# Pooling given out one VectorE instruction at a time, under four merge-gate tiles per layer instead of two

## The chip, the cores and the metric

One Trainium2 chip, one of its cores. The time is that of one execution of the whole program on the device, in microseconds (us); a kernel's time is the median of its runs. Engines: TensorE does matmuls (PE in the rows; PEld is its weight load), VectorE is DVE, ScalarE is ACT, GpSimd is POOL, and SyncE (SP) issues the DMAs.

## The reference

Two layers over 1024 latent tokens and 256 context tokens of width 1024, all in float32. A layer normalises its input, multiplies it by one wide matrix `w_in`, and cuts the product into the inputs of four branches, into gates, and into merge gates:

```
z      = split_cols(h @ w_in)            # pool_in, MLA, diff, windowed q/k/v, gates, merge
y_pool = for each of 4 column groups of 64, window w in (2, 4, 8, 16):
           mean of u over the window, minus u, then @ w_pool[group]; times s_pool
y_mla, y_diff, y_swa = three attentions
m      = sum over branches r of sigmoid(merge[r]) * ((y[r] * silu(gates[r])) @ w_br[r])
x      = x + gate * rms_norm(m @ w_out)
```

Layer 0 does this for all 1280 tokens, layer 1 for the 1024 latents (its keys and values still take all 1280).

## The kernel before, in words

**Precision.** A float32 product is three matmuls: each operand is split into a rounded part (ScalarE) and what is left of it (a subtraction on VectorE, for most weight tiles on GpSimd); `mm3` (line 74) issues high by high, high by low, low by high.

**Dense tiles.** `h @ w_in` is done in tiles of 128 output columns. A tile runs over chunks of tokens (512, 512, 256, or 512, 512), each of 8 steps of three matmuls into one of two PSUM buffers `pd`; then ScalarE copies the chunk out. `Dense` (line 319) holds a queue of such tiles in a fixed order. `fill(us)` (line 359) takes steps from the queue until their estimated cost covers `us`; a step of 512 tokens is put at 0.648, one of 256 at 0.324. So a tile is 12.96 of the planner's units over 1280 tokens and 10.37 over 1024. Where the queue is empty, `fill` does nothing. `until(name)` (line 368) runs the queue without a break up to the end of one tile. As a tile starts, the DMA of the next one's weights (512 KB) is issued; their split (rounding on ScalarE, subtraction `wl` on GpSimd) is issued at the next attention unit (line 1252).

**Later work.** `Later` (line 154) holds generators. Every dense step advances its clock by the step's cost, and a generator whose time has come is resumed; what it yields is the delay to its next part. `drain` runs it to its end.

**Order of the queue.** Values, keys and queries of the differential attention, which are run ahead of all attention by `until(W_DQ + 1)` (line 975); then eight gate tiles, the values (SV), keys (SK) and queries (SQ, two tiles) of the windowed attention, the pooling, and two merge-gate tiles (lines 788 to 800). These are given out between the pieces of attention.

**Attention** (lines 1245 to 1275). Units in the order differential, MLA, windowed. A unit has two or four score pieces (matmuls, a row minimum on VectorE, an exponential on ScalarE) and up to five turns (transposes on TensorE, `th` on ScalarE, `tl` on VectorE, matmuls into `acc`). After each piece `fill(f)` gives dense steps; `f` comes from `FILL` and `TURNS`. Ahead of the first piece stand 15 units of dense work in layer 0 and 13 in layer 1. `prefetch(i + 1)`, after a unit's first score piece, issues the DMAs of the next unit's keys, values and queries. For a windowed unit it first calls `dense.until(W_SQ + 1)` if SQ's second tile is not through yet (lines 1220 to 1223):

```python
if key[0] == 3:
    if any(it[0] == W_SQ + 1 for it in dense.items) or dense.gen and dense.name == W_SQ + 1:
        dense.until(W_SQ + 1)
    vals.drain()
```

**Rope.** SQ's second tile, like DQ's, hands each chunk to a chain: two products on VectorE and two on GpSimd, sums on VectorE, rounding on ScalarE, subtraction on VectorE, and four DMAs to DRAM (`ev2`, line 646), from where `prefetch` loads the queries.

**Pooling** (`pooled`, line 724). Two tiles of `pool_in`, each copied to `up` in SBUF; after each tile an item of the queue without a matmul tile, `rest`: for a chunk, window sums by two or four additions, a 64-partition copy, a product with `rcnt` (1 / count, by DMA), a subtraction, the split, and one `mm3` with `w_pool`. It yields twice per chunk, 0.3 and 0.4 units, so a whole chunk is given out at one or two places.

**Merge stage** (lines 1425 to 1476). For each branch r and output tile d the merge-gate tile is projected and the branch product of the tile before is computed and added. A tile in `early` was projected in the attention stage, kept in DRAM (`zmd`), and here is only loaded and put through a sigmoid (`reload`).

The engines' queues run in the order written into the program; a scheduler arranges that order ahead of time from this code's order and from its own estimate of when each instruction can start.

Of the kernel before, what the change touches and what calls it, by code (L numbers as in the profile page):

```python
# [8 lines left out]
F = mybir.dt.float32  # L9
R = mybir.dt.float32r  # L10
# [9 lines left out]
T = SEQ + CTX  # L20
# [12 lines left out]
def kernel(ctx: ExitStack, tc: tile.TileContext, A: dict, out: bass.AP):  # L33
# [46 lines left out]
    def dense_ps(n, m=128):  # L80
        return ps_d.tile([128, 512], F, name="pd", tag="pd")[0:m, 0:n]
# [28 lines left out]
    zmd = dram.tile([2, 128, T], F, name="zmd")  # L110
# [409 lines left out]
    def layer(l, es_prev):  # L520
# [84 lines left out]
        def f32(tag, n):  # L605
            return p2.tile([128, {"t1": 528, "t2": 528}.get(tag, 512)], F, name=tag, tag=tag, bufs=3 if tag == "tab" else 2)[:, 0:n]
# [6 lines left out]
        def spl(src, dh, dl, scale=None):  # L613
            pp = slice(0, src.shape[0])
            n = src.shape[-1]
            hi = p2.tile([128, 512], R, name="sh", tag="sh")[pp, 0:n]
            lo = p2.tile([128, 512], R, name="sl", tag="sl")[pp, 0:n]
            if scale is None:
                act(hi, src)
                tt(lo, src, hi.bitcast(F), ALU.subtract)  # L620
            else:
                act(hi, src, scale=scale)
                stt(lo, src, scale, hi.bitcast(F), ALU.mult, ALU.subtract)
            dh(hi)
            dl(lo)
# [88 lines left out]
                dma(zgd[j, :, c0:c0 + n], z)  # L714
            dense.tile(st, W_G + j, qch, ev)

        def merge_gate(e, i):
            def ev(ps, c0, n):
                z = f32("zc", n)
                act(z, ps)  # L720
                dma(zmd[e, :, c0:c0 + n], z)
            dense.tile(st, i, qch, ev)

        def pooled():
            LP = 8 + SEQ + 8 + CTX + 8
            H_, L_ = slice(64, 128), slice(0, 64)
            wph = p2.tile([128, 2, 128], R, name="wph", bufs=1)
            wpl = p2.tile([128, 2, 128], R, name="wpl", bufs=1)
            spc = p2.tile([128, 2], F, name="spc", bufs=1)
            keep = {}  # L730

            def pos(c0):
                return c0 + 8 if c0 < SEQ else c0 + 16

            def weights():
                wpr = f32("zc", 256).rearrange("p (a b) -> p a b", a=2)
                nc.gpsimd.memset(wpr, 0.0)
                for g in range(4):
                    o = 64 * (g % 2)
                    dma(wpr[o:o + 64, g // 2, o:o + 64], A["w_pool"][l, g])  # L740
                split(wpr, wph, wpl)
                dma(spc, A["s_pool"][l].rearrange("(j p) -> p j", p=128))

            for j in range(2):
                def ev(ps, c0, n, j=j):
                    if c0 == 0:
                        vals.drain()
                        if j == 0:
                            weights()
                        keep[j] = p2.tile([128, LP], F, name="up", tag="zt1", bufs=1)  # L750
                        nc.gpsimd.memset(keep[j], 0.0)
                    act(keep[j][:, pos(c0):pos(c0) + n], ps)
                dense.tile(st, W_POOL + j, qch, ev)

                def rest(j=j):
                    for c0, n in qch:
                        up = keep[j][:, pos(c0) - 8:pos(c0) + n + 8]
                        w = n + 16
                        a = f32("t1", w)
                        b = f32("t2", w)  # L760
                        tt(a[:, 1:w], up[:, 0:w - 1], up[:, 1:w], ALU.add)
                        if j == 0:
                            tt(b[H_, 8:8 + n], a[H_, 7:7 + n], a[H_, 9:9 + n], ALU.add)
                        else:
                            tt(b[:, 2:w - 1], a[:, 1:w - 2], a[:, 3:w], ALU.add)
                            tt(a[:, 4:w - 3], b[:, 2:w - 5], b[:, 6:w - 1], ALU.add)
                            tt(b[H_, 8:8 + n], a[H_, 4:4 + n], a[H_, 12:12 + n], ALU.add)
                        yield 0.3 * n / 512
                        nc.vector.tensor_copy(out=b[L_, 8:8 + n], in_=a[L_, 8:8 + n])
                        rc = f32("tab", n)  # L770
                        dma(rc, A["rcnt"][j, :, c0:c0 + n])
                        t1 = f32("tab", n)
                        tt(t1, b[:, 8:8 + n], rc, ALU.mult)
                        tt(t1, t1, up[:, 8:8 + n], ALU.subtract)
                        hl_ = {}
                        spl(t1, lambda h: hl_.__setitem__(0, h), lambda h: hl_.__setitem__(1, h))
                        ps = dense_ps(n)
                        mm3(ps, lambda k: wph[:, j], lambda k: wpl[:, j], lambda k: hl_[0], lambda k: hl_[1], [0], 1)
                        yv = f32("zc", n)
                        act(yv, ps, scale=spc[:, j:j + 1])  # L780
                        dma(yd[0][j, :, c0:c0 + n], yv)
                        yield 0.4 * n / 512
                dense.add(f"pool{j}", None, rest)


        vals, ups = Later(), Later()
# [4 lines left out]
        roped(W_DQ, dqd.rearrange("m a d n -> a m d n"), qch, 32 ** -0.5, 8, 16, ("C32", "S32"))  # L791
        for j in range(8):
            gates(j)
        values(W_SV, svd, 0)
        keys_swa()
        roped(W_SQ, sqd, qch, 64 ** -0.5, 4, 32, ("C64", "S64"))
        pooled()
        early = [W_M + 26, W_M + 29]
        for e, i in enumerate(early):
            merge_gate(e, i)  # L800

        p1b = pool(f"mlb{l}", 1, es_m)

# [466 lines left out]
        while pend:  # L1270
            dense.fill(1.0)
            pend.pop(0)()
        dense.until(early[-1])
        es_a.close()
        es_p.close()

# [148 lines left out]
        for q, (r, d) in enumerate(order):  # L1425
            i = W_M + r * 8 + d
            if q + 1 == len(order):
                st.load((l, W_O), use=0)
            elif i not in early:
                st.load((l, i + 2 if i + 1 in early else i + 1))  # L1430
# [14 lines left out]
            def ev(ps, c0, n, sg_tile=sg_tile):  # L1445
                act(sg_tile(c0, n), ps, AF.Sigmoid)
# [13 lines left out]
            body = reload(early.index(i)) if i in early else st.body((l, i), qch, ev)  # L1460
            some(body, KT)
            if prev:
                if prev[1] == 0:
# [251 lines left out]
```

## Time and profile before

| | us |
|---|---|
| median of 3 runs (lowest to highest) | 2755.56 (2752.95 to 2758.76) |
| the profiled execution | 2752.83 |
| its span, first to last instruction | 2749.9 |
| TensorE busy in it | 2616.0 (95%) |
| VectorE, ScalarE, GpSimd busy | 1526.6, 1190.7, 801.2 |
| mean granted TensorE clock | 0.973 of full speed |

Attention runs from about 240 to 840 us in layer 0 and from about 1700 to 2220 us in layer 1; the merge stages follow them. A TensorE that is shown as busy can still be slow: where PEclk is below 1.00 in a stretch, part of it ran at the lower of two clocks, half of full speed.

### The profile page before, as it was taken

The numbers are of one execution on the slowest core, as the hardware profiler recorded it, in microseconds if no ns is written. First come the engines' busy times: TensorE is split into PE (matmuls) and PEld (weight loads), VectorE is DVE, ScalarE is ACT, GpSimd is POOL, SyncE is SP. The second block draws the span as 40 slices with busy tenths as digits, with TensorE's granted clock in tenths as the row PEclk, the third lists the DMA queues.
The fourth block names the chain that finished last, engine by engine and source line by source line (L and its number), as shares of the span: only waits on it lengthen the run. The fifth ranks groups of instructions, "written<-read, shape, count | busy, mean of one in ns | idle before, by whom it ended". The sixth has DMA issues, their size and how long they took to land. (4 is left out here: it accounts for less than half of the span.)

```text
span 2749.9 us, 38514 instructions
## 1 busy us (share of the span) xinstructions
PE 2616.0 (95%) x14194; PEld 2205.1 (80%) x14194; DVE 1526.6 (56%) x2638; ACT 1190.7 (43%) x2188; POOL 801.2 (29%) x492
## 2 busy tenths in 40 slices
PE   7998999999999998999999998999998999999998
PEld 5777878888888887888878776888887878888878
DVE  7544778656665686333147653888666642222333
ACT  4433666655474221222245442776554742222231
POOL 4223433111000223444323322443010013344424
PEclk9998999999999999999999998999999999999999
DMA  6376333433334553222125366433433333322223
GB/s 238 103 198 208 116 96 92 115 118 115 94 109 122 170 182 124 77 77 66 54 92 179 101 205 207 133 94 106 136 100 94 112 118 98 98 79 79 79 73 100
DMA packets 211950, 327.00 MB, mean 119 GB/s; under 512 B 27060, under 2 KB 124466, under 8 KB 211762
## 3 DMA queue, kind: packets, MB, share of 16 engines
q1 hardware_dynamic: 211762, 324.55, 38.0%
q8 instruction: 111, 1.82, 0.3%
q14 instruction: 77, 0.63, 0.1%
HBM read 241.43 MB, written 80.22 MB: 117 GB/s over the span
## 5 line engine op out<-in xcount | busy, mean ns | idle before, releaser
L76 PE MATMUL pd<-h,wh 128*128 128x512 f32 (+2 forms) x2288 | 863.1, 377 | 24.6 <-ACT sg L50 11.9
L78 PE MATMUL pd<-h,wl 128*128 128x512 f32 (+2 forms) x2288 | 847.9, 371 | 0.4 <-POOL wl L53 0.4
L77 PE MATMUL pd<-h,wh 128*128 128x512 f32 (+2 forms) x2288 | 846.1, 370 | 0.0
L53 POOL TENSOR_TENSOR wl<-wraw,wh 128x1024 fp32r<-128x1024 f32 x106 | 260.7, 2459 | 926.3 <-ACT wh L50 886.2
L76 PEld LDWEIGHTS pd<-h,wh 128*128 128x128 f32 (+1 forms) x2288 | 437.0, 191 | 87.4 <-ACT sg L50 12.9
L78 PEld LDWEIGHTS pd<-h,wl 128*128 128x128 f32 (+1 forms) x2288 | 435.4, 190 | 70.2 <-POOL wl L53 1.8
L77 PEld LDWEIGHTS pd<-h,wh 128*128 128x128 f32 (+1 forms) x2288 | 437.3, 191 | 57.8 <-DVE h L56 0.8
L998 DVE CUSTOM_DVE_ANT_0 P<-pss,zero 128x1280 f32<-128x1280 f32 (+1 forms) x216 | 295.8, 1370 | 147.0 <-PE pss L1137 75.7
L53 DVE TENSOR_TENSOR tl<-pt,th 128x512 fp32r<-128x512 f32 (+1 forms) x420 | 277.0, 671 | 149.9 <-ACT th L50 146.4
L50 ACT ACTIVATE th<-pt 128x512 fp32r<-128x512 f32 (+1 forms) x420 | 239.6, 581 | 141.8 <-PE pt L1026 136.4
L1026 PE MATMUL pt<-kc,P 128*128 128x128 f32 x1632 | 256.6, 276 | 6.1 <-POOL P L53 1.6
L53 DVE TENSOR_TENSOR sg<-sg,pt 128x512 f32<-128x512 f32 x96 | 65.7, 687 | 349.9 <-PE pt L78 349.4
L1042 PE MATMUL acc<-th,vt 128*128 128x256 f32 x816 | 240.9, 309 | 7.5 <-ACT ot L50 6.6
L1042 PE MATMUL acc<-tl,vt 128*128 128x256 f32 x816 | 219.5, 290 | 16.6 <-DVE tl L53 16.5
L50 ACT ACTIVATE wh<-wraw 128x1024 fp32r<-128x1024 f32 x124 | 130.7, 1054 | 208.7 <-PE pd L77 139.1
L50 ACT ACTIVATE P<-P,m 128x1280 f32<-128x1280 f32 (+1 forms) x144 | 182.8, 1269 | 62.5 <-DVE m L998 62.0
L1026 PEld LDWEIGHTS pt<-kc,P 128*128 128x128 f32 x1632 | 191.6, 141 | 19.1 <-DVE P L56 5.4
L50 ACT ACTIVATE sg<-pd 128x512 f32<-128x512 f32 x120 | 70.9, 591 | 277.4 <-PE pd L78 269.3
L50 ACT ACTIVATE P<-P,negm 128x1280 f32<-128x1280 f32 (+3 forms) x144 | 146.6, 1018 | 95.0 <-DVE negm L998 94.0
L1042 PEld LDWEIGHTS acc<-th,vt 128*128 128x128 f32 x816 | 156.2, 191 | 39.0 <-ACT th L50 18.2
L53 POOL TENSOR_TENSOR m<-m,sg 128x512 f32<-128x512 f32 x96 | 131.0, 1371 | 190.8 <-DVE sg L53 189.9
L1042 PEld LDWEIGHTS acc<-tl,vt 128*128 128x128 f32 x816 | 156.2, 191 | 34.5 <-DVE tl L53 25.7
(293 smaller groups left out, 3946.5 us busy)
## 6 DMA issues: line engine op xcount, KB each, us to landing
wraw<-in_w_in_dram SPq DMA_DIRECT2D x108, 512.0 KB, 3.6
wmt<-in_w_modt_dram SPq DMA_DIRECT2D x64, 256.0 KB, 3.1
wraw<-in_w_out_dram SPq DMA_DIRECT2D x32, 512.0 KB, 3.3
yd<-ot SPq DMA_DIRECT2D x108, 128.0 KB, 2.0
kt<-dkd SPq DMA_DIRECT2D x64, 160.0 KB, 3.9
qt<-dqd SPq DMA_DIRECT2D x72, 128.0 KB, 2.8
ya<-yd SPq DMA_DIRECT2D x36, 256.0 KB, 3.1
yb<-yd SPq DMA_DIRECT2D x36, 256.0 KB, 3.0
```

The costliest lines, as they stand in the source:

```text
L50: return nc.scalar.activation(out=o, in_=i, func=func, **kw)
L53: return (e or nc.vector).tensor_tensor(out=o, in0=a, in1=b, op=op)
L76: nc.tensor.matmul(ps, wh(k), xh(k), start=k == 0, stop=False)
L77: nc.tensor.matmul(ps, wh(k), xl(k), start=False, stop=False)
L78: nc.tensor.matmul(ps, wl(k), xh(k), start=False, stop=k == n - 1)
L998: nc.vector.tensor_tensor_reduce(out=o, in0=i, in1=zero.to_broadcast([128, nk]) if mask is None else mask, scale=-1.0, scalar=1e30 if h is ...
L1026: t = nc.tensor.transpose(pt[:, 2 * j + i, :], Ps[i][:, (g + j) * 128:(g + j + 1) * 128], ident)
L1042: nc.tensor.matmul(acc, vt[:, kts[g + j], :], x[:, j, :], start=g + j == 0 and a == 0, stop=g + j == nk - 1 and a == 1)
```

## The change

The pooling tiles move up behind the gates, each followed by a merge-gate tile; SV, SK and SQ come after them and two more merge-gate tiles last. `early` becomes (3,2), (3,4), (3,6) and (2,2) instead of (3,2) and (3,5). `rest` becomes a generator in `vals` that starts when the pooling tile is through; it yields after every VectorE instruction, 0.7 units for 512 tokens, so it is given out under the steps of the merge-gate tile. The copy of 64 partitions goes from VectorE to ScalarE. The load of `rcnt` is issued at the chunk's start.

```diff
@@ merge_gate, pooled
-        def merge_gate(e, i):
+        def merge_gate(e):
+            i = W_M + 8 * early[e][0] + early[e][1]
...
-        def pooled():
+        pw = {}
+
+        def pooled(j):
...
-            for j in range(2):
-                def ev(ps, c0, n, j=j):
...
-                    act(keep[j][:, pos(c0):pos(c0) + n], ps)
-                dense.tile(st, W_POOL + j, qch, ev)
-
-                def rest(j=j):
-                    for c0, n in qch:
...
-                        tt(a[:, 1:w], up[:, 0:w - 1], up[:, 1:w], ALU.add)
...
-                            tt(b[H_, 8:8 + n], a[H_, 4:4 + n], a[H_, 12:12 + n], ALU.add)
-                        yield 0.3 * n / 512
-                        nc.vector.tensor_copy(out=b[L_, 8:8 + n], in_=a[L_, 8:8 + n])
-                        rc = f32("tab", n)
-                        dma(rc, A["rcnt"][j, :, c0:c0 + n])
...
-                        yield 0.4 * n / 512
-                dense.add(f"pool{j}", None, rest)
+            def ev(ps, c0, n):
+                if c0 == 0:
+                    vals.drain()
+                    if j == 0:
+                        weights()
+                    keep[j] = p2.tile([128, LP], F, name="up", tag="zt1", bufs=1)
+                    nc.gpsimd.memset(keep[j], 0.0)
+                act(keep[j][:, pos(c0):pos(c0) + n], ps)
+                if (c0, n) == qch[-1]:
+                    vals.add(rest(), 1.0)
+            dense.tile(st, W_POOL + j, qch, ev)
+
+            def rest():
+                for c0, n in qch:
+                    u = 0.7 * n / 512
...
+                    rc = f32("tab", n)
+                    dma(rc, A["rcnt"][j, :, c0:c0 + n])
+                    tt(a[:, 1:w], up[:, 0:w - 1], up[:, 1:w], ALU.add)
+                    yield u
+                    if j == 0:
+                        tt(b[H_, 8:8 + n], a[H_, 7:7 + n], a[H_, 9:9 + n], ALU.add)
+                        yield u
+                    else:
+                        tt(b[:, 2:w - 1], a[:, 1:w - 2], a[:, 3:w], ALU.add)
+                        yield u
+                        tt(a[:, 4:w - 3], b[:, 2:w - 5], b[:, 6:w - 1], ALU.add)
+                        yield u
+                        tt(b[H_, 8:8 + n], a[H_, 4:4 + n], a[H_, 12:12 + n], ALU.add)
+                        yield u
+                    act(b[L_, 8:8 + n], a[L_, 8:8 + n])
+                    t1 = f32("tab", n)
+                    tt(t1, b[:, 8:8 + n], rc, ALU.mult)
+                    yield u
+                    tt(t1, t1, up[:, 8:8 + n], ALU.subtract)
+                    yield u
+                    hl_ = {}
+                    spl(t1, lambda h: hl_.__setitem__(0, h), lambda h: hl_.__setitem__(1, h))
+                    yield u
+                    ps = dense_ps(n)
...
+                    mm3(ps, lambda k: wh_[:, j], lambda k: wl_[:, j], lambda k: hl_[0], lambda k: hl_[1], [0], 1)
...
+                    yield u
@@ order of the queue
+        early = [(3, 2), (3, 4), (3, 6), (2, 2)]
+        for j in range(2):
+            pooled(j)
+            merge_gate(j)
         values(W_SV, svd, 0)
         keys_swa()
         roped(W_SQ, sqd, qch, 64 ** -0.5, 4, 32, ("C64", "S64"))
-        pooled()
-        early = [W_M + 26, W_M + 29]
-        for e, i in enumerate(early):
-            merge_gate(e, i)
+        for e in range(2, len(early)):
+            merge_gate(e)
@@ end of the attention; merge stage: the same tests, by (r, d) instead of tile number
```

## Rows read from the trace of the kernel before

**Rows 1.** The page, part 1: busy us, share of the span, instructions, by engine.
```profile
PE 2616.0 (95%) x14194; PEld 2205.1 (80%) x14194; DVE 1526.6 (56%) x2638; ACT 1190.7 (43%) x2188; POOL 801.2 (29%) x492
```
**Rows 2.** Busy time by stretches, layer 0: stretch, us, engines, clock, DMA share, GB/s.
```profile
core 0: us, PE busy (x) PEld busy (x) DVE busy (x) ACT busy (x) POOL busy (x), PEclk, DMA share, GB/s
500.00:600.00 100.00, 99.48 (x629) 87.38 (x629) 59.38 (x99) 56.95 (x107) 8.08 (x5) 0.99 0.37 110
600.00:620.00 20.00, 18.05 (x97) 15.42 (x97) 10.91 (x15) 8.57 (x17) 3.05 (x2) 0.91 0.50 148
620.00:640.00 20.00, 17.48 (x113) 15.40 (x112) 17.23 (x25) 11.36 (x22) 8.21 (x7) 1.00 0.55 173
...
660.00:680.00 20.00, 17.31 (x104) 15.36 (x103) 15.87 (x26) 9.04 (x18) 2.37 (x1) 0.83 0.38 107
...
700.00:720.00 20.00, 17.74 (x124) 15.93 (x123) 16.11 (x23) 9.74 (x18) 2.81 (x1) 1.00 0.18 56
720.00:740.00 20.00, 17.43 (x81) 14.85 (x82) 11.65 (x26) 8.92 (x19) 0.00 (x0) 0.74 0.37 110
```
**Rows 3.** Busy time by stretches, layer 1, columns as before.
```profile
2020.00:2040.00 20.00, 18.25 (x103) 15.21 (x102) 15.57 (x21) 11.44 (x20) 6.53 (x4) 0.96 0.37 129
2040.00:2060.00 20.00, 20.00 (x121) 17.67 (x121) 9.73 (x14) 9.31 (x16) 0.00 (x0) 0.96 0.25 80
2060.00:2080.00 20.00, 16.02 (x89) 13.77 (x88) 16.75 (x24) 9.73 (x18) 3.55 (x2) 0.91 0.54 145
...
2100.00:2120.00 20.00, 15.83 (x75) 12.34 (x74) 17.20 (x27) 10.13 (x17) 2.38 (x1) 0.75 0.21 67
```
**Rows 4.** Timeline of VectorE: start, duration, line, tiles, shapes.
```profile
666.90 2.55 DVE L53 TENSOR_TENSOR t<-t 64x256 f32<-64x256 f32 x1
714.21 2.51 DVE L769 COPY t<-t 64x512 f32<-64x512 f32 x1
2104.27 2.44 DVE L53 TENSOR_TENSOR t<-up 128x527 f32<-128x527 f32 x1 [0.70 <-ACT up L50]
```
**Rows 5.** Timeline of GpSimd in the same stretches.
```profile
666.81 2.37 POOL L53 TENSOR_TENSOR wl<-wraw,wh 128x1024 fp32r<-128x1024 f32 x1 [31.12 <-ACT wh L50]
713.62 2.81 POOL L53 TENSOR_TENSOR wl<-wraw,wh 128x1024 fp32r<-128x1024 f32 x1 [29.63 <-ACT wh L50]
2103.77 2.38 POOL L53 TENSOR_TENSOR wl<-wraw,wh 128x1024 fp32r<-128x1024 f32 x1 [25.27 <-ACT wh L50]
```
**Rows 6.** Timeline of TensorE: matmuls ahead of which it idled, and the releaser.
```profile
670.41 0.58 PE L1042 MATMUL acc<-tl,vt 128*128 128x256 f32 x1 [1.85 <-DVE tl L53]
...
722.00 0.80 PE L76 MATMUL pd<-sh,wph 128*128 128x512 f32 x1 [1.39 <-ACT sh L50]
...
2068.36 0.39 PE L1042 MATMUL acc<-tl,vt 128*128 128x256 f32 x1 [2.39 <-DVE tl L53]
...
2114.87 0.79 PE L76 MATMUL pd<-sh,wph 128*128 128x512 f32 x1 [2.33 <-ACT sh L50]
```
**Rows 7.** Groups by form, 660 to 740 us: line, count, busy, mean ns, idle before.
```profile
L769 DVE COPY t<-t 64x512 f32<-64x512 f32 x4 | 3.8, 938 | 0.0
L53 DVE TENSOR_TENSOR t<-up 128x527 f32<-128x527 f32 x4 | 2.7, 702 | 0.0
L53 DVE TENSOR_TENSOR tab<-t,tab 128x512 f32<-128x512 f32 x4 | 2.7, 680 | 0.0
```
**Rows 8.** Timeline of TensorE, first score matmuls of the attention, layers 0 and 1.
```profile
247.59 1.41 PE L1137 MATMUL pss<-kt,qt 128*128 128x512 f32 x3 [6.93 <-DMA qt<-dqd]
...
1702.97 1.41 PE L1137 MATMUL pss<-kt,qt 128*128 128x512 f32 x3 [7.30 <-DMA qt<-dqd]
```
**Rows 9.** Busy time by stretches around the attention's start, columns as in rows 2.
```profile
240.00:260.00 20.00, 11.79 (x39) 8.54 (x38) 3.16 (x5) 3.96 (x6) 4.74 (x2) 0.66 0.72 232
1690.00:1710.00 20.00, 12.33 (x40) 8.48 (x39) 3.29 (x6) 5.59 (x8) 3.94 (x2) 0.76 0.82 255
```
**Rows 10.** Busy time by stretches: layer 0's merge stage with both reloaded tiles.
```profile
1300.00:1360.00 60.00, 60.00 (x314) 51.40 (x313) 12.52 (x21) 15.19 (x28) 25.00 (x19) 1.00 0.20 64
```

More of the change, by code (lines that the diff above doesn't have):

```diff
@@ L109 @@
     zgd = dram.tile([8, 128, T], F, name="zgd")
-    zmd = dram.tile([2, 128, T], F, name="zmd")
+    zmd = dram.tile([4, 128, T], F, name="zmd")
     mq = dram.tile([2, 4, 96, T], R, name="mq")
@@ L722, in merge_gate @@
             dense.tile(st, i, qch, ev)
-        def pooled():
+        pw = {}
+        def pooled(j):
             LP = 8 + SEQ + 8 + CTX + 8
             H_, L_ = slice(64, 128), slice(0, 64)
-            wph = p2.tile([128, 2, 128], R, name="wph", bufs=1)
-            wpl = p2.tile([128, 2, 128], R, name="wpl", bufs=1)
-            spc = p2.tile([128, 2], F, name="spc", bufs=1)
+            if j == 0:
+                pw.update(h=p2.tile([128, 2, 128], R, name="wph", bufs=1), l=p2.tile([128, 2, 128], R, name="wpl", bufs=1),
+                          s=p2.tile([128, 2], F, name="spc", bufs=1))
             keep = {}
@@ L740, in weights @@
                     dma(wpr[o:o + 64, g // 2, o:o + 64], A["w_pool"][l, g])
-                split(wpr, wph, wpl)
-                dma(spc, A["s_pool"][l].rearrange("(j p) -> p j", p=128))
-            for j in range(2):
-                def ev(ps, c0, n, j=j):
[L746 to L751, printed above, removed]
-                    act(keep[j][:, pos(c0):pos(c0) + n], ps)
-                dense.tile(st, W_POOL + j, qch, ev)
-                def rest(j=j):
-                    for c0, n in qch:
[L757 to L760, printed above, removed]
-                        tt(a[:, 1:w], up[:, 0:w - 1], up[:, 1:w], ALU.add)
[L762 to L766, printed above, removed]
-                            tt(b[H_, 8:8 + n], a[H_, 4:4 + n], a[H_, 12:12 + n], ALU.add)
-                        yield 0.3 * n / 512
-                        nc.vector.tensor_copy(out=b[L_, 8:8 + n], in_=a[L_, 8:8 + n])
-                        rc = f32("tab", n)
-                        dma(rc, A["rcnt"][j, :, c0:c0 + n])
[L772 to L781, printed above, removed]
-                        yield 0.4 * n / 512
-                dense.add(f"pool{j}", None, rest)
@@ new lines, in weights @@
+                split(wpr, pw["h"], pw["l"])
+                dma(pw["s"], A["s_pool"][l].rearrange("(j p) -> p j", p=128))
+            def ev(ps, c0, n):
[8 more added lines that the diff above has]
+                    vals.add(rest(), 1.0)
@@ new lines, in pooled @@
+            dense.tile(st, W_POOL + j, qch, ev)
+            def rest():
+                for c0, n in qch:
+                    u = 0.7 * n / 512
+                    up = keep[j][:, pos(c0) - 8:pos(c0) + n + 8]
+                    w = n + 16
+                    a = f32("t1", w)
+                    b = f32("t2", w)
+                    rc = f32("tab", n)
+                    dma(rc, A["rcnt"][j, :, c0:c0 + n])
+                    tt(a[:, 1:w], up[:, 0:w - 1], up[:, 1:w], ALU.add)
+                    yield u
+                    if j == 0:
+                        tt(b[H_, 8:8 + n], a[H_, 7:7 + n], a[H_, 9:9 + n], ALU.add)
[17 more added lines that the diff above has]
+                    ps = dense_ps(n)
+                    wh_, wl_ = pw["h"], pw["l"]
+                    mm3(ps, lambda k: wh_[:, j], lambda k: wl_[:, j], lambda k: hl_[0], lambda k: hl_[1], [0], 1)
+                    yv = f32("zc", n)
+                    act(yv, ps, scale=pw["s"][:, j:j + 1])
+                    dma(yd[0][j, :, c0:c0 + n], yv)
+                    yield u
@@ L1272, in layer @@
             pend.pop(0)()
-        dense.until(early[-1])
+        dense.until(W_M + 8 * early[-1][0] + early[-1][1])
         es_a.close()
@@ L1428, in layer @@
                 st.load((l, W_O), use=0)
-            elif i not in early:
-                st.load((l, i + 2 if i + 1 in early else i + 1))
+            elif (r, d) not in early:
+                st.load((l, i + 2 if order[q + 1] in early else i + 1))
             braw = tp.tile([128, 2, 128], F, name="braw", tag="braw", bufs=1)
@@ L1459, in layer @@
                 prep.add(gated_y(r, 1), 0.0)
-            body = reload(early.index(i)) if i in early else st.body((l, i), qch, ev)
+            body = reload(early.index((r, d))) if (r, d) in early else st.body((l, i), qch, ev)
             some(body, KT)
```

## The prediction

> **What bounds the kernel now.** I read the page first: TensorE is busy for 2616.0 of 2749.9 us [rows 1], so 133.9 us of idle time and whatever its clock loses are all that a reordering can win. Then I cut the two attention stages into stretches by the windows view and asked of each what TensorE lost: its idle time, plus (1 - PEclk) times the length, since half clock halves its work. A quiet stretch of the MLA units, 500 to 600 us, loses 0.52 + 1.0 = 1.5 us, or 0.3 per 20 us [rows 2]. That is the floor that I expect of any stretch with dense steps between attention pieces. The losses sit in clusters instead:
>
> - Pooling, layer 0: 660 to 680 loses 2.69 + 3.4 = 6.1; 700 to 720 2.3; 720 to 740 2.57 + 5.2 = 7.8; together 16.1 [rows 2]. Layer 1: 2060 to 2080 loses 3.98 + 1.8 = 5.8; 2100 to 2120 4.17 + 5.0 = 9.2; together 15.0 [rows 3]. Over the five stretches 31.1, less a floor of 1.5, is **29.6 us**.
> - SQ's rope, layer 0, 600 to 640: 3.75 + 2.5 = 6.3 [rows 2]; layer 1, 2020 to 2060: 2.55 + 0.8 = 3.35 [rows 3]. Less a floor of 1.2 that is **8.4 us**.
>
> The timelines say how. In the pooling clusters VectorE is at 16 to 17 us of 20 [rows 2, 3], against 59 of 100 in the quiet stretch. A pooling instruction that takes 0.4 to 0.7 us otherwise took 2.55, 2.51 and 2.44 [rows 4, 7], each while GpSimd subtracted a weight tile [rows 5]. Behind it in VectorE's queue stood the attention's `tl`, and TensorE waited for that: 1.85 and 2.39 us [rows 6]. Pooling's own matmuls sit in TensorE's queue straight behind a chain of five to seven VectorE instructions, and TensorE waited for them too: 1.39 and 2.33 [rows 6]. The half clock follows such waits.
>
> **The change, part by part.**
>
> *Pooling given out singly.* 60 VectorE instructions (36 in layer 0, 24 in layer 1, without the copies) move from ten bunches, with no dense step between, to one per dense step or so. The clusters go: 29.6 us is the whole that can be won here. What comes late instead? Two things. (a) The product waits for the copy, which is now on ScalarE, and the low part for the rounding there; VectorE's queue is in order, so a `tl` or a row minimum behind them waits too. Between 0 and 2.33, the longest wait for ScalarE [rows 6], each time. I take it near 0 for most: ScalarE is at 57% in the quiet stretch [rows 2], and the order is written with this hop in it. (b) The weight split. One `wl` of about 2.4 us [rows 5] runs per dense tile, and it will fall in a stretch where pooling is given out, since the next tile's split is issued at the next unit and a merge-gate tile spans several units. So four hits (two tiles, two layers). A hit costs between 0, if dense steps cover it, and 2.39 of waiting [rows 6] plus the 1.8 that the clock of 0.91 takes in that stretch [rows 3], 4.2. I take half, since one pooling instruction instead of a bunch now stands ahead of `tl`: 4 x 2.1 = **about 9 us stay** with a little of (a) in it. Bounds 0 and 35 (ten chunks of waits with their clock, below).
>
> The rows show the collision three times: a VectorE instruction that starts while `wl` runs is held until 0.3 to 0.6 us after `wl`'s end [rows 4, 5]. The Trainium skill, SBUF — State Buffer, "Who interferes with whom", says that a VectorE instruction with two SBUF inputs, or a copy in its two-port mode, contends with a GpSimd instruction that reads SBUF, and that whoever began first blocks the other for the whole instruction. By that rule, taking the copy off VectorE helps little: additions, product, subtraction and low part all have two SBUF inputs, and spreading them in time makes it likelier that each `wl` meets one. The trace agrees (an addition was held as long as the copy). If only the copy contended, the sum would come out 9 us better.
>
> *Two more merge-gate tiles per layer in the attention.* They leave a merge stage whose stretch with both reloaded tiles is busy for 60.00 of 60 us at full clock [rows 10], and add the same matmuls to the attention: nothing by itself, as TensorE bounds both. Their loads, sigmoids and stores lie beside that; (2,2), (3,4) and (3,6) stand between full tiles, as (3,2) and (3,5) did, so the next weights still have a tile's time to load. The moved tiles are worth something only as cover. But the planner's sums show that the cover per unit stays as it was: the fills up to the first windowed prefetch are about 185 units in layer 0 (15 ahead, 93 over the differential units, 77 over MLA's) and 154 in layer 1, in both kernels. The old `rest` used up 3.5 and 2.8 of all the fills without a matmul; that comes back as a shorter empty tail, which I count as nothing.
>
> *SQ becomes a block.* Up to SQ the new queue holds 14 tiles: 14 x 12.96 = 181 in layer 0, 12 x 10.37 + 2 x 12.96 = 150 in layer 1. So at the prefetch of the first windowed unit only about 4 units of SQ are done, and `until` runs the other 21 (layer 0) and 16 (layer 1) without a break. In the old queue SQ ends at 12 tiles, 156 units, and the call does nothing. Inside the block TensorE has dense work throughout and waits for no rope: the 8.4 us go. But at its end the rope of the last chunks, its DMAs, and behind them on SP's queue the keys, values and queries of the windowed unit are late, and only five turns, a score piece and some 4.7 units of fill stand ahead of the first windowed score. The nearest rows are the same thing at the attention's start, where DQ is run by `until`: TensorE waited 6.93 and 7.30 us for `qt` [rows 8], and the stretches lose 8.2 + 6.8 = 15.0 and 7.7 + 4.8 = 12.5 [rows 9]. So the price is between 0 (dense steps of the next merge-gate tile cover it) and 27.5 for both layers. I take half, **14 us**: four key loads instead of eight come ahead of `qt`, but there is also less to do than the 13 to 15 units ahead of the first score.
>
> *Sum.* 29.6 + 8.4 - 9 - 14 = 15 us gained. From the profiled execution's 2752.8 that is 2737.8; the median of the runs lies 2.7 above that execution, so 2740.5, say 2740. `rcnt` is loaded earlier on SP, the stores of `zmd` are a few more among hundreds: nothing.
>
> **Rivals.**
>
> - *All covered.* If dense steps cover the block's end and the weight splits, nearly all of the 38 is won, say 33: 2722. For it: the next merge-gate tile's weights are loaded during SQ's second tile, so its steps are ready. Against: at DQ's end a gate tile was there too, and TensorE still waited.
> - *The block costs what DQ's does.* 38 - 9 - 27.5 = 1.5 gained: 2754. For it: the same chain (rope on three engines, DRAM, SP in order) and less work ahead of the first score.
> - *VectorE's queue is now held inside MLA (slower).* Each of the ten chunks puts a wait for ScalarE or GpSimd ahead of a `tl`, in the units where TensorE was quiet; it decides from the point where a chunk costs over 2.4 us (38 - 14 = 24 over ten). At 1.85 [rows 6] plus the 1.7 that half of the 3.4 clock loss of 660 to 680 gives [rows 2], 3.55 each: 35.5, so 38 - 35.5 - 14 = 11.5 lost: 2767. Against: ten chunks would each have to be unlucky, while VectorE has 40 of 100 us free there [rows 2].
> - *It doesn't do what it says:* merge-gate tiles left over at the end of attention would run there uncovered by pieces. By the sums the queue still empties some 9 and 13 units of fill before the end, so this would change nothing anyway; 2740 with the rest as above.
>
> **How the numbers follow.** Forecast 0.50, all covered 0.15, block as DQ's 0.20, queue held 0.13, not as said 0.02. Within 0.2% (5.5 us either way) is about what a measurement can't tell from no change: 2750 to 2761. Faster: 0.15 + 0.48 of the forecast + 0.05 of the block's case = 0.68. Within: 0.12 of the block's case, 0.05 from the others = 0.17. Slower: 0.15. The range leaves a tenth on each side: 2721 (all covered) to 2760 (half of the way from the block's case to the held queue).
>
> **What would show it.** Right: no stretch with VectorE above 16 of 20 us in MLA; pooling's matmuls (`pd<-sh,wph`) without waits over 1 us; dense matmuls without a break for 11 us or more shortly before the first windowed score, then a wait for `qt<-sqd` with a dip of the clock; merge stages shorter by two tiles each. Wrong: new waits of TensorE for `tl` in every unit that carries pooling, or a wait at the block's end as long as DQ's; the first would make the held queue true, the second the block's case. A time under 2725 would mean that I saw costs at the block's end that dense steps cover.

## The result, and the profile after

The changed kernel takes 2718.06 us (median of 4 runs, 2715.78 to 2725.88) against 2754.26 (4 runs, 2745.72 to 2758.76): ratio 0.9882, 95% interval 0.9863 to 0.9901, so 1.2% faster, 32 to 36 us. I had forecast 2740 with a range of 2721 to 2760: the direction held, the gain is about twice the 15 us that I summed, and the time lies under the range.

The page, part 1, of the changed kernel, as in [rows 1]; its span is 2723.1 us against 2749.9:

```profile
PE 2601.1 (96%) x14194; PEld 2198.2 (81%) x14194; DVE 1530.5 (56%) x2628; ACT 1200.1 (44%) x2208; POOL 804.3 (30%) x492
```

The count of matmuls is the same; TensorE idles 122.0 us instead of 133.9, and spends less time at half clock. To see where, I cut both spans into three stages: MLA units and windowed units, each from its first score matmul, and the merge stage from its first sigmoid on ScalarE, for layer 0 and then layer 1. The windows view of the kernel before by these stages (columns as in [rows 2]):

```profile
497.20:740.10 242.90, 230.00 (x1385) 201.06 (x1386) 153.54 (x249) 128.00 (x239) 25.70 (x17) 0.95 0.37 111
740.10:844.10 104.00, 98.56 (x665) 89.09 (x664) 63.31 (x142) 73.58 (x171) 4.79 (x2) 0.97 0.35 102
844.10:1389.60 545.50, 531.64 (x2755) 454.69 (x2754) 267.56 (x532) 130.15 (x235) 180.24 (x118) 0.99 0.34 108
1915.90:2131.80 215.90, 204.72 (x1208) 176.17 (x1207) 139.23 (x205) 112.68 (x198) 25.23 (x16) 0.96 0.36 110
2131.80:2221.80 90.00, 88.03 (x601) 78.49 (x600) 59.66 (x125) 63.96 (x147) 4.78 (x2) 1.00 0.34 99
2221.80:2638.70 416.90, 415.38 (x1834) 341.10 (x1834) 125.30 (x176) 112.55 (x186) 154.66 (x88) 1.00 0.30 94
```

and of the changed kernel:

```profile
504.10:755.00 250.90, 244.53 (x1522) 217.32 (x1521) 150.04 (x239) 134.63 (x250) 29.66 (x17) 0.99 0.38 116
755.00:856.80 101.80, 98.75 (x668) 89.01 (x667) 63.53 (x142) 73.57 (x172) 4.79 (x2) 0.98 0.38 110
856.80:1371.40 514.60, 502.50 (x2609) 429.56 (x2608) 266.52 (x532) 128.27 (x233) 175.33 (x116) 0.99 0.37 115
1903.00:2125.70 222.70, 217.15 (x1308) 189.84 (x1308) 136.81 (x201) 119.16 (x210) 27.71 (x15) 0.99 0.38 116
2125.70:2216.90 91.20, 89.16 (x607) 79.86 (x606) 59.82 (x126) 63.81 (x147) 4.78 (x2) 1.00 0.36 102
2216.90:2611.90 395.00, 393.50 (x1737) 323.01 (x1736) 125.81 (x174) 109.92 (x184) 150.00 (x86) 1.00 0.32 99
```

With the prediction's loss (idle plus (1 - PEclk) times the length), MLA lost 25.0 and 19.8 us and now loses 8.9 and 7.8: 28.1 less. The windowed units and the merge stages lose 5.5 less together. (The clock has two decimals, so each number is good to 1 or 2 us.) The merge stages are 52.8 us shorter; MLA and windowed units, which took these matmuls in, are only 13.8 longer. The span fell by 26.8 us; the medians differ by more, as the profiled execution of the changed kernel lay 7.8 above its own median. In it MLA of layer 0 begins 6.9 us later, behind stages that the change hardly touches.

The windows of the changed kernel, in MLA and at the end of the attention:

```profile
500.00:520.00 20.00, 18.57 (x117) 15.98 (x116) 19.73 (x33) 12.20 (x25) 3.52 (x3) 1.00 0.54 161
520.00:590.00 70.00, 70.00 (x451) 62.73 (x450) 40.36 (x64) 40.30 (x72) 3.57 (x2) 1.00 0.27 84
590.00:610.00 20.00, 18.30 (x118) 16.30 (x117) 17.33 (x30) 12.59 (x26) 2.38 (x1) 1.00 0.40 121
610.00:640.00 30.00, 30.00 (x193) 27.09 (x192) 15.02 (x21) 15.70 (x27) 2.39 (x1) 1.00 0.45 141
640.00:740.00 100.00, 99.66 (x615) 88.27 (x615) 51.76 (x83) 48.57 (x93) 17.14 (x10) 1.00 0.39 116
740.00:760.00 20.00, 15.67 (x90) 13.75 (x89) 12.87 (x21) 9.29 (x20) 4.18 (x3) 0.83 0.63 191
760.00:820.00 60.00, 60.00 (x420) 55.27 (x420) 37.77 (x83) 41.61 (x101) 2.40 (x1) 1.00 0.39 109
820.00:840.00 20.00, 18.53 (x134) 16.29 (x132) 15.07 (x34) 17.74 (x37) 2.39 (x1) 1.00 0.44 134
840.00:860.00 20.00, 18.42 (x96) 15.35 (x95) 8.57 (x22) 12.38 (x31) 0.00 (x0) 0.91 0.34 105
...
2110.00:2130.00 20.00, 15.79 (x93) 13.80 (x92) 13.00 (x18) 8.18 (x16) 5.25 (x3) 0.91 0.58 186
```

Where the clusters of [rows 2] stood, TensorE is now busy without a gap at full clock. Two things are left: short hits at 500 and 600 us, and one loss per layer at the end of the SQ block (740 to 760, 2110 to 2130). In layer 0 the windowed units lose some more from 820 us on. The timeline of VectorE, GpSimd and TensorE of the changed kernel shows the first two: first a hit, then the block's end in layer 0 and in layer 1.

```profile
596.87 2.74 DVE L53 TENSOR_TENSOR tab<-t,tab 128x512 f32<-128x512 f32 x1
596.68 2.38 POOL L53 TENSOR_TENSOR wl<-wraw,wh 128x1024 fp32r<-128x1024 f32 x1 [37.13 <-ACT wh L50]
601.47 0.39 PE L1057 MATMUL acc<-tl,vt 128*128 128x256 f32 x1 [1.70 <-DVE tl L53]
...
743.11 2.89 DVE L53 TENSOR_TENSOR t<-t,t 128x256 f32<-128x256 f32 x2
745.93 0.68 DVE L53 TENSOR_TENSOR tl<-pt,th 128x512 fp32r<-128x512 f32 x1
742.87 2.52 POOL L53 TENSOR_TENSOR wl<-wraw,wh 128x1024 fp32r<-128x1024 f32 x1
746.66 0.58 PE L1057 MATMUL acc<-tl,vt 128*128 128x256 f32 x1 [3.80 <-DVE tl L53]
...
2110.24 2.67 DVE L53 TENSOR_TENSOR t<-zc,tab 128x512 f32<-128x512 f32 x1
2109.81 2.56 POOL L53 TENSOR_TENSOR wl<-wraw,wh 128x1024 fp32r<-128x1024 f32 x1 [2.89 <-ACT wh L50]
2117.06 0.39 PE L1057 MATMUL acc<-tl,vt 128*128 128x256 f32 x1 [4.21 <-DVE tl L53]
```

The collision of [rows 4, 5] is in all three: a sum or product on VectorE whose inputs both lie in SBUF, started while GpSimd subtracts `wl`, ends only after it, and `tl` stands behind. `tl` itself, one of whose inputs is TensorE's result `pt`, is not held: at 666.25 us one took 0.69, all of it beside a `wl` of 665.54 to 667.94. At the block's end the rope of SQ's last chunks is what collides. The block itself runs as forecast, dense matmuls without a break from 714.4 to 738.6 us; behind SQ's last step (737.2) only four steps of the next tile run, the last at 741.0, ahead of the matmul that waits.

### The profile page after: what moved, and what is told of

It reads as the page before. It is cut to its first block, busy times and chain, and to the rows that moved or that the text cites. A ratio compares the mean times of both kernels' runs of the same rounds, so it can differ in the third digit from the quotient of the medians.

```text
span 2723.1 us, 38568 instructions
## 1 busy us (share of the span) xinstructions
PE 2601.1 (96%) x14194; PEld 2198.2 (81%) x14194; DVE 1530.5 (56%) x2628; ACT 1200.1 (44%) x2208; POOL 804.3 (30%) x492
## 5 line engine op out<-in xcount | busy, mean ns | idle before, releaser
L1057 PE MATMUL acc<-tl,vt 128*128 128x256 f32 x816 | 218.0, 288 | 17.4 <-DVE tl L53 17.1
```

What stands on the lines that cost most here:

```text
L1057: nc.tensor.matmul(acc, vt[:, kts[g + j], :], x[:, j, :], start=g + j == 0 and a == 0, stop=g + j == nk - 1 and a == 1)
```

## The experiments

The same kernel before was run beside each; its medians were 2750.50 us (beside *again*, *bunch*, *count*, *spread*), 2748.74 (*two*, *inqueue*, *cover*, *noblock*) and 2752.97 (the others). Ratios are to it. The theory that I brought: TensorE loses where dense matmuls run out beside a chain on VectorE, so cover is what pays; the rival was the prediction's own, waits in VectorE's queue whose number and place decide.

**again**: the changed kernel once more.

> The changed kernel unchanged, for its spread and a second trace. If the 7 us by which the stretches before MLA in layer 0 (pre-stage and differential units, unchanged code), and 5 us in layer 1, were longer in its first trace are chance, this trace has the span 8 to 12 us shorter at most (about 2711 to 2716) or the same scatter in other places; the ratio to the kernel before stays near 0.988. If they belong to the change, they come again.

2715.67 us (2713.23 to 2721.79), ratio 0.9880 (0.9861 to 0.9900). The result stands. Of the delays ahead of MLA a part came again: in layer 0 MLA starts at 501.3 us (504.1 in the first trace, 497.2 in the kernel before); in layer 1 the time from the end of merge to MLA is 5.2 us longer than in the kernel before, where the first trace had 5.3.

**bunch**: each chunk of pooling given out at two places instead of one instruction at a time; all other `yield u` of a chunk go.

```diff
                     tt(a[:, 1:w], up[:, 0:w - 1], up[:, 1:w], ALU.add)
-                    yield u
...
                         tt(b[H_, 8:8 + n], a[H_, 7:7 + n], a[H_, 9:9 + n], ALU.add)
-                        yield u
+                        yield 2 * u
...
                         tt(b[H_, 8:8 + n], a[H_, 4:4 + n], a[H_, 12:12 + n], ALU.add)
-                        yield u
+                        yield 4 * u
...
                     dma(yd[0][j, :, c0:c0 + n], yv)
-                    yield u
+                    yield 4 * u
```

> Changed kernel, but each chunk of pooling is given out at two places again (additions; then copy, product, subtraction, split and matmuls), with the same total delay, under the same merge-gate tiles. Theory of the waits (the gain comes from not bunching VectorE work ahead of TensorE's): TensorE waits on tl and on sh/sl of pooling again, 12 to 25 us of the gain go, 2730 to 2743. Rival, the cover (the gain comes from matmul steps of the merge-gate tiles standing beside the pooling, whatever its grain): within 6 us of the changed kernel, 2712 to 2726.

2714.14 us (2713.32 to 2715.28), ratio 0.9870 (0.9851 to 0.9890). The rival, the cover, held. Giving out singly is worth nothing that can be measured: two to four VectorE instructions at one place hurt no more than one, once a merge-gate tile runs beside them.

**count**: the kernel before with four early merge-gate tiles; its order and bunched pooling stay (the DRAM buffer `zmd` grows with them).

```diff
-        early = [W_M + 26, W_M + 29]
+        early = [W_M + 26, W_M + 28, W_M + 30, W_M + 18]
```

> Kernel before, pooling in bunches and queue order as before, but four merge-gate tiles per layer projected in the attention instead of two. Theory of the waits: moved matmuls are worth nothing by themselves, pooling clusters stay: 2748 to 2758, no change from before. Rival, the cover: the two more tiles fill idle time at the end of the windowed units, 10 to 20 us faster than before, 2735 to 2745.

2729.98 us (2727.34 to 2732.43), ratio 0.9927 (0.9910 to 0.9945): 20.5 us from two more tiles alone, slightly more than the cover's theory had, and far from the theory of the waits. The kernel before lost time where its queue had run dry, at the end of the windowed units and the start of the merge stage, by its windows:

```profile
820.00:840.00 20.00, 15.19 (x88) 13.03 (x87) 10.51 (x27) 16.68 (x36) 0.00 (x0) 0.83 0.31 97
...
860.00:880.00 20.00, 18.07 (x91) 14.92 (x90) 9.60 (x16) 4.75 (x9) 2.39 (x1) 0.91 0.46 141
```

That is 8.2 and 3.7 us. With four tiles, the same view of this kernel:

```profile
720.00:740.00 20.00, 16.67 (x75) 13.92 (x76) 13.85 (x30) 8.67 (x18) 0.00 (x0) 0.74 0.40 128
...
800.00:860.00 60.00, 60.00 (x389) 53.58 (x389) 35.13 (x77) 40.01 (x92) 4.79 (x2) 1.00 0.40 123
860.00:880.00 20.00, 20.00 (x101) 16.98 (x100) 6.28 (x11) 6.86 (x13) 4.97 (x2) 1.00 0.61 200
```

The tail is full and the merge stage starts without a wait, while pooling's cluster at 720 is as bad as before (3.3 + 5.2 = 8.5). By the stages used above, windowed units and merge stages of both layers lose 13.8 us here instead of 31.4; MLA loses as much as before (44.6 and 44.9).

**spread**: the changed kernel in the old order with two early tiles, so that only the way of giving out pooling is changed (with it the copy, which stays on ScalarE, and the earlier load of `rcnt`).

```diff
-        early = [(3, 2), (3, 4), (3, 6), (2, 2)]
-        for j in range(2):
-            pooled(j)
-            merge_gate(j)
+        early = [(3, 2), (3, 5)]
         values(W_SV, svd, 0)
...
-        for e in range(2, len(early)):
-            merge_gate(e)
+        for j in range(2):
+            pooled(j)
+            merge_gate(j)
```

> Changed kernel with the old queue order and the old two early tiles (SV, SK, SQ, then pooling and merge-gate tile twice): only the single giving out and the copy on ScalarE are left of the change, and there is no block of SQ. Theory of the waits: pooling clusters mostly go, SQ's rope clusters stay and no block's end: 15 to 29 us faster than before, 2725 to 2740; pooling of the second tile that is drained at the windowed prefetch keeps some. Rival, the cover: with two tiles only, 2748 to 2756.

2737.93 us (10 runs, 2732.22 to 2743.29), ratio 0.9956 (0.9940 to 0.9972): 12.6 us. That is inside the range of the theory of the waits and outside the cover's, which had no gain without more tiles. MLA is shorter by 16.4 and 12.0 us, but the windowed units are longer by 5.0 and 5.7. The windows of this kernel show the tail empty sooner:

```profile
640.00:740.00 100.00, 98.75 (x646) 88.97 (x645) 60.16 (x99) 56.22 (x107) 6.03 (x3) 1.00 0.32 95
...
780.00:800.00 20.00, 14.51 (x92) 11.28 (x91) 8.70 (x19) 13.46 (x27) 2.37 (x1) 0.98 0.59 170
800.00:820.00 20.00, 18.88 (x119) 16.86 (x119) 14.78 (x30) 15.13 (x37) 0.00 (x0) 0.85 0.17 50
```

So pooling's clusters are won, and part of the gain is given back where the queue has run dry. The two parts alone, 20.5 and 12.6, make up the change's 32 to 36 within the intervals.

**two**: the changed kernel and its order with (3,2) and (3,5) alone.

```diff
-        early = [(3, 2), (3, 4), (3, 6), (2, 2)]
+        early = [(3, 2), (3, 5)]
```

> The changed kernel with two early merge-gate tiles, (3,2) and (3,5), as before; the new order and the pooling given out singly stay. Theory A (the two tiles are worth some 20 us wherever they are run, because the queue then lasts through the windowed units and the merge stage starts without an uncovered stretch): 2732 to 2740, the loss in the last windowed units and in the first 20 us of merge. Theory B (my prediction's step: the tiles are worth nothing by themselves, and what the four tiles gave in the old order was only cover for the pooling): 2714 to 2720.

2743.69 us (12 runs, 2741.19 to 2750.06), ratio 0.9982 (0.9970 to 0.9994), some 28 us behind the changed kernel: theory A, and past its range. In this order both tiles are used up ahead of SQ, and nothing follows it; the windows of this kernel:

```profile
740.00:800.00 60.00, 50.15 (x312) 42.48 (x313) 38.93 (x85) 40.83 (x95) 0.55 (x1) 0.90 0.44 126
800.00:840.00 40.00, 37.17 (x243) 30.71 (x242) 29.79 (x67) 31.00 (x76) 0.00 (x0) 0.96 0.22 64
```

The windowed units lose 15.9 + 4.4 = 20.3 us here without a dense step beside them. VectorE and ScalarE are at 0.65 and 0.68 of the first stretch: no engine is full, the chain between the pieces is bare.

**inqueue**: the changed kernel, with pooling an item of the queue again, without matmuls of another tile beside it; it yields at two places per chunk, as in the kernel before.

```diff
-                if (c0, n) == qch[-1]:
-                    vals.add(rest(), 1.0)
...
+            dense.add(f"pool{j}", None, rest)
```

> The changed kernel with its order and its four tiles, but pooling as an item of the dense queue again, without matmuls of its own tile between (3.5 and 2.8 units of fill go to it), two places per chunk; the copy back stays on ScalarE. Theory A (what the change gives is that dense matmuls run while pooling's VectorE chain does; an item without matmuls leaves TensorE bare for its length): the clusters of the kernel before come back, 10 to 20 us: 2726 to 2736. Theory B (the order and four tiles suffice, the pooling's place is worth little): 2714 to 2722.

2741.67 us (12 runs, 2736.91 to 2749.89), ratio 0.9973 (0.9960 to 0.9986): theory A, at a higher price than it asked, some 26 us. The clusters are back, by the windows of this kernel:

```profile
500.00:520.00 20.00, 16.85 (x96) 14.39 (x95) 18.58 (x31) 11.86 (x24) 3.21 (x3) 0.91 0.56 166
600.00:620.00 20.00, 16.88 (x95) 14.59 (x94) 16.30 (x27) 11.30 (x24) 2.36 (x1) 0.91 0.51 156
...
1980.00:2000.00 20.00, 14.03 (x75) 11.43 (x74) 16.94 (x24) 10.63 (x20) 2.80 (x1) 0.85 0.35 110
```

One of pooling's own matmuls waits 5.14 us there:

```profile
1995.70 0.79 PE L76 MATMUL pd<-sh,wph 128*128 128x512 f32 x1 [5.14 <-ACT sh L50]
```

One rival is left by the edit alone: as an item, pooling might also be packed closer in time. The traces answer it. From the first addition of a pooling tile to its last low part, the four tiles (two per layer) take 32.4, 24.4, 23.8 and 17.1 us in the changed kernel, 29.4, 21.5, 24.1 and 17.6 in *bunch*, 30.7, 23.9, 25.7 and 14.9 here, and 26.0, 26.2, 16.8 and 16.1 in the kernel before. What differs is the dense matmuls (`pd<-h`) in these stretches, 127, 121, 45 and 63, and TensorE's idle time in them, 6.5, 6.1, 17.3 and 16.0 us. The fourth stretch in the windows of the changed kernel, with 27 dense matmuls, and of this one, with none:

```profile
1970.55:1987.65 17.10, 16.98 (x102) 14.52 (x101) 16.97 (x27) 10.33 (x18) 2.71 (x1) 1.00 0.39 129
1986.39:2001.33 14.94, 8.97 (x44) 7.12 (x43) 14.38 (x21) 7.80 (x13) 2.80 (x1) 0.77 0.38 121
```

So what pays in the giving-out is neither the grain nor a wider spread of VectorE's work, but that pooling no longer occupies a place of the dense queue.

**cover**: 6 units of the next tile directly behind the SQ block.

```diff
                         dense.until(W_SQ + 1)
+                        dense.fill(6.0)
```

> The changed kernel with one more call: right behind the SQ block, ahead of the prefetch's transfers, 6 units of the next merge-gate tile run. The two block ends lose 13.1 us in the changed kernel's trace, most of it TensorE waiting for `tl` behind the rope on VectorE (3.80 and 4.21 us) and half clock behind it. Theory A (the wait is paid because no dense step stands between the rope and the first windowed softmax pieces): 6 units, about 6 us of dense work per layer, outlast both waits, so 8 to 12 us go: 2703 to 2711. Theory B (VectorE is behind by its own queue and the same dense steps are then missing a few units later, or in the windowed tail): 2713 to 2722.

2715.35 us (2709.75 to 2719.71), ratio 0.9874 (0.9854 to 0.9894): no gain, theory B. The windows of this kernel:

```profile
740.00:760.00 20.00, 19.13 (x138) 17.57 (x137) 12.47 (x23) 10.00 (x21) 1.80 (x1) 1.00 0.63 181
800.00:820.00 20.00, 15.75 (x86) 12.78 (x85) 10.14 (x22) 14.45 (x30) 2.36 (x1) 0.83 0.52 147
820.00:840.00 20.00, 18.35 (x123) 16.43 (x123) 14.41 (x31) 14.30 (x34) 0.00 (x0) 0.91 0.21 60
840.00:860.00 20.00, 19.21 (x106) 15.70 (x106) 10.00 (x26) 12.60 (x31) 0.00 (x0) 1.00 0.37 115
```

The block's end falls from 7.7 to 0.9 us. The collision itself is still there (two sums of 256 tokens take 2.95 us at 739.47, beside a `wl` of 2.58), but with dense steps in its queue TensorE hardly waits for it (0.17 us). The tail, 800 to 860, rises from 4.9 to 7.65 + 3.45 + 0.79 = 11.9. What is won at one place is lost 60 us later; in layer 1 MLA and windowed units together are 1.1 us shorter. The queue is a store of cover, and the 6 units can be spent once.

**noblock**: more fill per MLA unit, so that SQ is done ahead of the prefetch.

```diff
-    FILL = ({1: 4.75, 2: 4.9, 3: 1.5, "n": 1.5, "uk": 1.2, "uq": 1.5, "uv": 2.0, "pre": 15.0},
-            {1: 4.5, 2: 4.6, 3: 1.5, "n": 2.5, "uk": 1.2, "uq": 1.5, "uv": 2.0, "pre": 13.0})
+    FILL = ({1: 6.1, 2: 4.9, 3: 1.5, "n": 1.5, "uk": 1.2, "uq": 1.5, "uv": 2.0, "pre": 15.0},
+            {1: 5.65, 2: 4.6, 3: 1.5, "n": 2.5, "uk": 1.2, "uq": 1.5, "uv": 2.0, "pre": 13.0})
```

> The changed kernel with more fill per MLA unit in attention (6.1 instead of 4.75 in layer 0, 5.65 instead of 4.5 in layer 1), so that SQ is done by its steps before the first windowed unit is prefetched and nothing is run as a block. Theory A (the block's end is a loss of its own): its 13.1 us go, the waits for SQ's rope between the units come back in part (8.4 us in the kernel before), 2706 to 2716. Theory B (more dense work between the pieces only delays the attention, the queue empties sooner and the windowed tail runs uncovered, as in the kernel before, where 820 to 840 us lost 8.8 us): 2718 to 2730.

2724.75 us (6 runs, 2721.31 to 2736.45), ratio 0.9916 (0.9894 to 0.9937): slower than the changed kernel by 7 to 9 us by the medians, though the intervals of the ratios just touch. The time lies in theory B's range; its reason, a bare tail, is only partly there (the windowed units of layer 0 lose 7.7 us in this trace instead of 5.1). Theory A's premise failed too, since without a block TensorE still waits for `tl` behind SQ's rope and a `wl`. The timeline of this kernel, of which the slowest execution (2736.45 us) was profiled:

```profile
748.82 0.58 PE L1057 MATMUL acc<-tl,vt 128*128 128x256 f32 x1 [2.86 <-DVE tl L53]
```

**spread4**: the changed kernel with four tiles in the old order (SV, SK, SQ, then pooling and merge-gate tiles), so without a block.

```diff
         early = [(3, 2), (3, 4), (3, 6), (2, 2)]
-        for j in range(2):
-            pooled(j)
-            merge_gate(j)
         values(W_SV, svd, 0)
...
+        for j in range(2):
+            pooled(j)
+            merge_gate(j)
         for e in range(2, len(early)):
             merge_gate(e)
```

> The changed kernel with all four early merge-gate tiles and the pooling given out singly, but in the old place: values, keys and SQ first, then the pooling tiles, so no SQ block. Against the kernel before, two early tiles alone gave 20.5 us (2729.98) and giving out alone 12.6 us (2737.93). Theory A (the two add, and the order itself gives nothing): 2714 to 2722. Theory B (the new order has a part of its own, because pooling then ends before the windowed units and its left-over is not drained at their prefetch): 2724 to 2732. Theory C (the block's end, 13 us in the changed kernel, is what is avoided): 2702 to 2711.

2713.14 us (2710.99 to 2715.35), ratio 0.9861 (0.9839 to 0.9882): the changed kernel's time within the intervals, just under theory A's range. The order and the SQ block, on which I spent 22 us of the sum in both directions, are together worth nothing that the intervals show, once there are four tiles; by the ratios alone the old order would be some 5 us faster.

**five**: a fifth early tile, (2,5); `zmd` grows to five.

```diff
-        early = [(3, 2), (3, 4), (3, 6), (2, 2)]
+        early = [(3, 2), (3, 4), (3, 6), (2, 2), (2, 5)]
```

> The changed kernel with a fifth early merge-gate tile, (2,5). Its matmuls leave the merge stage (about 13.9 us in layer 0, 11.2 in layer 1) and lengthen the attention by what the idle time of the last windowed units doesn't take. In the changed kernel the queue empties 9.1 and 13.1 units before the end, and 820 to 860 us and 2180 to 2220 us lose 10.5 and 8.0 us against their own matmuls' time. Theory A (early tiles are worth what uncovered tail they fill): 5 to 12 us, 2704 to 2711. Theory B (the last windowed units are held by VectorE and ScalarE, and the fifth tile runs behind them): 2713 to 2720.

2703.28 us (2699.39 to 2707.20), ratio 0.9825 (0.9802 to 0.9847): another 12 to 15 us, theory A and a little more. The tail is full; the block's end stays, by this kernel's windows:

```profile
740.00:760.00 20.00, 17.48 (x102) 16.02 (x103) 11.78 (x22) 8.37 (x18) 1.58 (x1) 0.83 0.55 157
760.00:860.00 100.00, 99.75 (x678) 90.72 (x677) 58.46 (x131) 68.63 (x164) 7.20 (x3) 1.00 0.37 107
```

**fivecover**: both, the fifth tile and the 6 units behind the block.

> The fifth tile together with the 6 units behind the SQ block. In the kernel with the cover alone the waits for `tl` at the block's end went, and with them the half clock there, yet the time stayed (2715.35) as the last windowed units then had 6 units less. Theory A (there is a store of dense units, and a cover is worth something only where the store lasts): with a fifth tile both are covered, 2698 to 2708, at least 4 us under the fifth tile alone. Theory B (cover and tail are not what holds the stage): 2711 to 2720.

2698.32 us (2695.17 to 2701.31), ratio 0.9807 (0.9784 to 0.9830): the fastest of all, 55 us below the kernel before and 17 to 20 below the changed one. Over *five* it is 5.0 us; the intervals of the two ratios overlap, but this kernel's windows show what went:

```profile
740.00:760.00 20.00, 19.80 (x146) 18.25 (x145) 11.83 (x25) 12.11 (x27) 2.17 (x2) 1.00 0.62 174
760.00:860.00 100.00, 99.91 (x676) 90.41 (x675) 58.46 (x130) 67.80 (x162) 5.39 (x3) 1.00 0.39 117
```

The same 6 units that bought nothing in *cover* now keep TensorE busy from the block to the end of the windowed units, 0.3 us lost in 120.

**dvecopy**: the copy back on VectorE.

```diff
-                    act(b[L_, 8:8 + n], a[L_, 8:8 + n])
+                    nc.vector.tensor_copy(out=b[L_, 8:8 + n], in_=a[L_, 8:8 + n])
```

> The changed kernel with the copy back in the pooling on VectorE as before, ten copies in all over both layers. Theory A (VectorE is not what bounds a stretch with dense steps, and the hop over ScalarE costs nothing either): no difference, 2712 to 2721. Theory B (the copy holds VectorE's queue while GpSimd writes a weight tile, about 2.5 us at a hit): 2718 to 2728.

2721.30 us (2718.82 to 2722.18), ratio 0.9888 (0.9863 to 0.9912): by the ratio the changed kernel's 0.9880 and 0.9882; by the median 3 to 6 us more, just outside theory A's range and inside theory B's. So a few us stay open.

## Why the prediction was wrong

- **Pooling's clusters, 29.6 us, go**: right. No stretch of [rows 2, 3] is left, and pooling's matmuls wait for nothing. The reason that I gave, that the work is spread singly, is not it: *bunch* has the same time, *inqueue* loses it, and in the trace the work is hardly spread wider than in the kernel before (97.6 us for the four tiles against 85.0). (VectorE "at 16 to 17 us of 20" was not true of 720 to 740, which shows 11.65.)
- **9 us of them stay, four hits**: too much. There were two, 1.43 and 1.70 us of TensorE (503 and 601 us), at a granted clock of 1.00, so 3.1 us. Of the rest one met a pooling addition (1973 us, 1.50 us) under running matmuls, the others none.
- **The 8.4 us of SQ's rope go and the block's end costs 14**: the sizes agree with the trace, the cause of the second is not the one I gave. 740 to 760 loses 4.3 + 3.4, 2110 to 2130 4.2 + 1.8, together 13.7. But TensorE waits for `tl` behind the rope on VectorE, not for `qt<-sqd`. That `wl` lengthens this wait is read from the trace; no run moved it alone. *cover* shows that dense steps behind the block take the wait away.
- **The floor of MLA stays**: a smaller miss. I kept 0.3 us per 20; 520 to 590 and 610 to 640 lose nothing by the windows.
- **Not foreseen**: the differential units of layer 1, in whose last one pooling is now given out, are 4.2 us longer (212.9 to 217.1), in *again* and *bunch* too, but not in *five* (213.2). In the first trace a pooling addition took 3.46 us there (1898.10), beside a GpSimd product `P` of 2.92; *again*, as long, has no such hit. The cause stays open.
- **"The moved tiles are worth something only as cover", and the shorter empty tail, "which I count as nothing"**: this is the step that failed. I argued that TensorE bounds the attention and the merge stage alike, from one full stretch of merge [rows 10], and did not look at the end of the windowed units. There the queue was dry, and the rows shown under *count* were to be had. The term that I put at 0 measured 20.5 us (*count*). I even had the two numbers that say it, 9 and 13 units of fill missing at the end, and used them only to dismiss a rival.

Term by term, the runs give: giving out with two tiles, 29.6 - 9 = 20.6 in the sum, 12.6 measured (*spread*), as the windowed units then run dry sooner; the tiles, 0 in the sum, 20.5 measured (*count*); order and block, 8.4 - 14 = -5.6 in the sum, some 5 us of loss by the ratios of *spread4* and the changed kernel, which the intervals don't part from nothing. So one term was 8 us too high and another 20 too low, and the first hid part of the second.

Against my sum for MLA, 38 - 9 - 14 = 15, stand 28.1 measured there: 38 - 1.7 (one hit of the two lies in MLA) - 13.1 (the block's 13.7 less its floor) = 23.2, and about 5 more from floor and rest. Windowed units and merge stages add 5.5. That this is so little beside *count*'s 20.5 fits the store: in the changed kernel the added tiles cover pooling first and the tail with what is left, and a fifth tile still won 12 to 15.

Of the rivals, "all covered" had the nearest time, 2722, for a wrong reason: the block's end is not covered. The sentence "under 2725 would mean that I saw costs at the block's end that dense steps cover" is false by the rows above; covering it (*cover*) changed nothing in the time. VectorE's held queue fell: it is at 19.73 and 17.33 of 20 us in two stretches, and TensorE loses 1.4 and 1.7 there.

The Trainium skill, SBUF — State Buffer, "Who interferes with whom", says that a VectorE instruction with two SBUF inputs contends with a GpSimd instruction that reads SBUF, and that the port pair that they share is an exclusive lock. The trace agrees (2.74 us beside a `wl` of 2.38, 2.89 beside 2.52). The use that I made of it, that freeing VectorE of the copy helps little, is not contradicted by *dvecopy*, which leaves room for a few us. The other use, that spreading the work makes hits likelier, was not borne out: the work was hardly spread, and two hits cost TensorE time instead of four.

## What to carry to other kernels

Where independent matmuls are given out between the pieces of a latency-bound chain, count them as a store: ask where the store runs dry, and value each further tile by the bare stretches that are left, at full loss including the half clock behind them. A cover moved from one gap to another won nothing here until the store lasted to the end. Side work on VectorE belongs beside such tiles, not in their queue.

## What the runs showed of the hardware beyond what I had expected

A wait of TensorE does not always cost clock: after 1.43 and 1.70 us the granted clock stayed at 1.00, while after the 3.80 and 4.21 at the block's end 740 to 760 shows 0.83 and 2110 to 2130 0.91. The length of a wait alone does not tell it: in the kernel before, 660 to 680 with its wait of 1.85 us shows 0.83, and 720 to 740 with 1.39 shows 0.74 [rows 2, 6]. And GpSimd's weight split delays VectorE even where VectorE's instruction is short: two 256-token sums took 2.89 us beside a `wl` of 2.52, while two 512-token sums just ahead (738.72 us) took 1.28.
